# A gain row spread by TensorE, loads in fixed order and zero products in the opening stage of a hybrid decoder layer

## The chip, the cores and the metric

The kernel runs on one core of one Trainium2 chip. The metric is the device time of one execution in microseconds (us). TensorE does the matrix products, VectorE (DVE) and ScalarE (ACT) the elementwise work, GpSimd (POOL) a few small steps, SyncE (SP) issues most of the loads and stores.

## The reference, cut to what matters

The layer takes x, 1024 tokens by 1024 features, in float32. Only its beginning is touched by the change.

```
h    = rms_norm(x, norm_mix_pre)          # x * rsqrt(mean(x*x) + 1e-6) * gain
proj = h @ w_in                           # q, k, v | B, C, xc | g_att, g_conv
y_att  = stick_breaking_attention(q, k, v) @ w_att_branch
y_conv = (B * causal_dwconv(C * xc)) @ w_conv_branch
x = x + rms_norm((sigmoid(g_att)*y_att + sigmoid(g_conv)*y_conv) @ w_out, norm_mix_post)
# then a convolutional feed-forward part with norms of its own (w_up, w_down)
```

The columns of `w_in` for v are 512; for each of q and k they are 512 as well.

## The kernel before, in words

Float32 operands are represented by pairs of float16 numbers: a high half, and a low half that holds what the high half leaves out. One exact product of such pairs is made of three float16 products: high by high, high by low and low by high (`PASSES`). Before a tensor is split it is multiplied by a power of two, so that it fits float16. For weights the power comes from the sum of squares of the weight: `scale_of` adds up the partial sums, a product with a matrix of ones (into tile `pr`, line 76) spreads the total over the partitions, and three small DVE instructions make the power (lines 78 to 81). For the normalised input the power comes from the largest gain (`gain_max`, line 187, and `gain_pow2`, lines 194 to 197).

The opening stage of `mixer` works on eight token tiles of 128 tokens (tt = 0 to 7, called x0 to x7 as loads) and on four weight tiles of v (`st[0]` to `st[3]`, called v0 to v3 as loads; 128 by 1024 float32, 512 KB each). For a token tile the steps are:

- `load_x`: a DMA from SP's queue, 512 KB.
- `square_x`: ACT squares and sums (line 58); `rstd_x`: one DVE instruction (line 181) and a power on POOL (line 182).
- `norm_x`: DVE multiplies the tile by its reciprocal root and by the gain (line 359). The gain is `gb`, a 128 by 1024 tile that a DMA fills by reading the gain's 4 KB row once for each partition (line 407, 512 KB written).
- `turn_x`: eight transposes of 128 by 128 on TensorE into PSUM (line 364). The PSUM pool for them has two buffers.
- `high` (ACT, line 367) and `low` (DVE, line 370): the two halves of the turned tile, written to `hT`. "high(3)" is that step for token tile 3.

For v: ACT and DVE square the four weight tiles (`sm_v`; lines 58 and 480), `scale_of` gives the scale, `w_high` (ACT, line 431) and `w_low` (DVE, line 434) make the two halves `wv`, and `v_pass` (line 427) issues the products for a token tile into a PSUM bank `pv`. `v_out` evicts such a bank. Inside the stage the weights of q and k are begun too: `square_w` loads and squares them, `open_w` takes the scale and casts them. The first q and k products (`pq`, `pk`, line 211) end the stage; the attention stage follows, and after it the gates, the output projection and the feed-forward part.

The order of TensorE, DVE and ACT instructions in the opening stage and in the attention stage is the order in which the program names them (`tc.manual_schedule`, lines 466 and 918). Outside those stretches, and on SP before the change, a planner in the compiler chooses the order by priorities and a timeline that it simulates. Each engine runs its queue in order. SP's loads stand in the queue as x0, the gain, v0, x1, v1, v2, v3, x2, x3, two small weights of the convolutions, x4 to x7.

## Time and profile before

| what | us |
|---|---|
| median of 3 runs | 1352.25 |
| lowest and highest of them | 1351.61, 1354.85 |
| the profiled execution, whole | 1350.92 |
| the profiled execution, its span from first to last instruction | 1349.2 |

The profile is of one execution. Times in its rows are counted from the span's start. In a row of the timeline the columns are: start, duration, engine, line of the program and operation, the tile written and the tiles read with their shapes, a count, and in brackets how long the engine had been idle before and what ended the wait. PE is TensorE's product, PEld its weight load, SPq an issue of a DMA on SP's queue. A row of the windows holds the stretch, its length, the busy time (with the number of instructions) of PE, PEld, DVE, ACT and POOL, the granted TensorE clock, the share of time in which the DMA engines were busy, and GB/s.

### The profile page before, as it was taken

Reading aid. Unit: us, or ns where it says so; the run is one execution under the profiler, and the core shown is the slowest. Engines: PE = TensorE matmul, PEld = TensorE weight load, DVE = VectorE, ACT = ScalarE, POOL = GpSimd, SP = SyncE. Lnnn points to the kernel's source line nnn. Section 1 sums busy time; section 2 is a strip of 40 time slices with the busy share of each in tenths; the row PEclk is TensorE's granted clock in tenths of the full one; section 3 lists DMA queues with packets and bytes.
Section 4 is the critical chain, followed back from the end, with each engine's and each line's share of the span. In section 5 each row is a group of like instructions: output and inputs, shape, how many; then the busy total and the mean of one; then the engine's idle time right before and its main releaser. Section 6 shows DMA issues by size and latency. Waiting matters only on the chain. (4 is left out here: it accounts for less than half of the span.)

```text
span 1349.2 us, 16783 instructions
## 1 busy us (share of the span) xinstructions
PE 1311.9 (97%) x6491; PEld 590.0 (44%) x6491; DVE 1050.8 (78%) x1697; ACT 859.1 (64%) x1205; POOL 34.5 (3%) x58
## 2 busy tenths in 40 slices
PE   5999999999998999999999999999999999999997
PEld 3544444344433444444444444444444444444443
DVE  6568887878878957878788977975894896699855
ACT  6578877877777966665555676743752762576524
POOL 2000000000000000000110000000000000000002
PEclk9999999999999999999999999999999999999999
DMA  7011201101001222241431123222220312313126
GB/s 267 33 33 32 63 32 32 36 28 48 32 16 32 63 63 66 76 177 57 137 114 44 51 63 126 63 63 94 63 94 1 125 63 63 125 34 123 63 48 109
DMA packets 26608, 96.12 MB, mean 71 GB/s; under 512 B 3088, under 2 KB 3216, under 8 KB 26528
## 3 DMA queue, kind: packets, MB, share of 16 engines
q1 hardware_dynamic: 25088, 89.80, 20.2%
q0 software_dynamic: 1440, 5.24, 2.1%
q8 instruction: 51, 0.84, 0.3%
q14 instruction: 29, 0.24, 0.1%
HBM read 86.61 MB, written 8.42 MB: 70 GB/s over the span
## 5 line engine op out<-in xcount | busy, mean ns | idle before, releaser
L1538 PEld LDWEIGHTS <-wh_u 128*128 128x128 f16 x1848 | 178.8, 98 | 217.6 <-issue 3.8
L1312 PE MATMUL pd<-wdh,f 128*128 128x512 f16 (+1 forms) x1068 | 230.2, 377 | 2.7 <-ACT wdh L97 1.1
L1312 PEld LDWEIGHTS <-f 128*128 128x128 f16 x1068 | 104.5, 98 | 126.9 <-issue 4.0
L97 ACT ACTIVATE wh_u<-ws_u,sc 128x1024 f16<-128x1024 f32 (+1 forms) x66 | 64.7, 999 | 103.6 <-DVE sc L80 80.0
L1319 DVE SCALAR_TENSOR_TENSOR yacc<-pd,sd,yacc 128x512 f32<-128x512 f32 (+1 forms) x81 | 58.6, 742 | 73.4 <-PE pd L1312 65.9
L1538 PEld LDWEIGHTS <-wh_g 128*128 128x128 f16 x588 | 56.9, 98 | 68.7 <-issue 0.4
L1123 PE MATMUL py<-wh_wo,m 128*128 128x512 f16 x384 | 83.9, 379 | 0.0
L98 DVE SCALAR_TENSOR_TENSOR wh_u<-ws_u,sc,wh_u 128x1024 f16<-128x1024 f32 (+1 forms) x66 | 72.4, 1103 | 9.5 <-ACT wh_u L97 9.4
L824 ACT ACTIVATE sh<-sp 128x1024 f16<-128x1024 f32 (+3 forms) x48 | 40.4, 841 | 53.4 <-DVE sp L819 53.1
L1615 DVE SCALAR_TENSOR_TENSOR ugu<-cgu,cw_g,ugu 128x1023 f32<-128x1023 f32 (+1 forms) x44 | 56.4, 1283 | 11.3 <-ACT ugu L1613 10.9
L828 DVE TENSOR_TENSOR sh<-sp,sh 128x1024 f16<-128x1024 f32 (+3 forms) x48 | 45.9, 956 | 18.0 <-ACT sh L824 17.8
L1615 DVE SCALAR_TENSOR_TENSOR ua<-cau,cw_a,ua 128x1023 f32<-128x1023 f32 (+1 forms) x44 | 56.3, 1280 | 1.4 <-ACT ua L1613 1.3
L1123 PEld LDWEIGHTS <-m 128*128 128x128 f16 x384 | 37.5, 98 | 44.1
L819 DVE TENSOR_TENSOR sp<-A,sp 1x1024 f32<-1x1024 f32 (+3 forms) x40 | 35.9, 897 | 25.4 <-PE A L781 21.7
L850 ACT ACTIVATE w<-e 128x1024 f16<-128x1024 f32 (+3 forms) x48 | 40.5, 843 | 21.3 <-DVE e L845 20.4
L854 DVE SCALAR_TENSOR_TENSOR w<-e,w 128x1024 f16<-128x1024 f32 (+3 forms) x48 | 45.8, 954 | 9.2 <-ACT w L850 9.2
L814 ACT ACTIVATE sp<-e,one 128x1024 f32<-128x1024 f32 (+3 forms) x48 | 44.4, 925 | 6.0 <-DVE e L809 3.1
L845 DVE TENSOR_TENSOR e<-e,g 128x1024 f32<-128x1024 f32 (+3 forms) x48 | 45.7, 953 | 1.9 <-ACT g L841 1.8
L58 ACT ACTIVATE jk_u<-ws_u 128x1024 bf16<-128x1024 f32 x44 | 46.4, 1054 | 0.8
L756 PE MATMUL pywc<-p,wh_wc 128*128 128x512 f16 x192 | 43.2, 379 | 3.5 <-ACT sga L730 1.1
L211 PE MATMUL pcb<-hT,wh_cb 128*128 128x512 f16 x192 | 44.9, 379 | 0.9 <-DVE sc_cb L89 0.8
L800 ACT ACTIVATE e<-z,cz 128x1024 f32<-128x1024 f32 (+3 forms) x48 | 43.0, 897 | 3.6 <-PE z L781 3.6
(697 smaller groups left out, 2623.3 us busy)
## 6 DMA issues: line engine op xcount, KB each, us to landing
ws_u<-w_up_nt SPq DMA_DIRECT2D x44, 512.0 KB
ds<-w_down SPq DMA_DIRECT2D x22, 512.0 KB
wd<-w_down SPq DMA_DIRECT2D x22, 512.0 KB
ws_g<-w_in_nt SPq DMA_DIRECT2D x14, 512.0 KB
x<-x SPq DMA_DIRECT2D x8, 512.0 KB
ws_wo<-w_out SPq DMA_DIRECT2D x8, 512.0 KB
xr<-x SPq DMA_DIRECT2D x8, 512.0 KB
out<-x SPq DMA_DIRECT2D x7, 512.0 KB
```

Of the source, the lines that this page charges most:

```text
L58: self.nc.scalar.activation(self.junk(f"jk_{name}"), src, AF.Square, accum_out=acc)
L97: self.nc.scalar.activation(dst[:, 0, :], src, AF.Copy, scale=s)
L98: self.nc.vector.scalar_tensor_tensor(dst[:, 1, :], src, s, dst[:, 0, :], ALU.mult, ALU.subtract)
L211: nc.tensor.matmul(ps, w[:, wi, ds(k * P, P)], hT[:, hi, k, ds(c * NH, NH)], start=n == 0, stop=n == last)
L828: nc.vector.tensor_tensor(sh[:, 1, :, off:], u["sp"][:, :, off:], sh[:, 0, :, off:], ALU.subtract)
L845: nc.vector.tensor_tensor(e[:, :, off:], e[:, :, off:], u["g"][:, :, off:], ALU.mult)
L854: nc.vector.scalar_tensor_tensor(w[:, 1, :, off:], u["e"][:, :, off:], 2.0 ** 14, w[:, 0, :, off:], ALU.mult, ALU.subtract)
L1123: nc.tensor.matmul(ps, m16[k][:, hi, ds(tt * P, P)], wo[k][:, wi, sl], start=k == 0 and p == 0, stop=k == 7 and p == 2)
L1312: nc.tensor.matmul(pd[nh], f16[g][k][:, hi, ds(tt * P, P)], w[k][:, wi, ds(*part)], start=run is runs[0] and n == 0, stop=run is runs[-1] ...
L1319: nc.vector.scalar_tensor_tensor(y[:, sl], ps, sm[:, 0:1], y[:, sl], ALU.mult, ALU.add)
L1538: nc.tensor.matmul(ps, w[wt][:, wi, ds(wc * NH + k * P, P)], self.block(i, hi, k), start=first and n == 0, stop=n == 3 * KH - 1, skip_grou ...
L1615: nc.vector.scalar_tensor_tensor(u[:, lag:], c[:, :T - lag], sm[:, 2 - lag:3 - lag], u[:, lag:], ALU.mult, ALU.add)
```

## The change

- The gain's row goes to one partition (`g_row`, 4 KB, a DMA on ACT's queue, ahead of ACT's table load). TensorE spreads it over 128 partitions by two float32 products with a row of ones into a PSUM tile `gp`, which takes one of the two buffers for turned tiles. The norms of token tiles 0 and 1 read `gp`; the others read `gb` as before.
- The powers of two of the gain are made on one partition and spread by a further product (`ps2`).
- SP's loads get a fixed order, and the broadcast into `gb` stands behind x2.
- `warm(n)` issues n products of zeros, 128 by 512, into a bank that nobody reads: 3 ahead of turn 0, 1 on each side of turn 1, 4 behind the product of v's scale.
- The squares of v2 and v3 are split between ACT (first 512 columns) and DVE (the others).
- The high half of the first weight tile is cast in two halves, and the products of the high weight halves are put in another order (token tile 1's products with its low half one weight later).
- The cast of the constant `tri` moves from the start of the program to between low(0) and low(1).
- The products of token tiles 2 and 3 are cut in two: the first 12 of the 24 stand ahead of the q weight's or the k weight's scale product.

```diff
-            nc.scalar.preload_act_table_set("natural_log_exp_and_others")
...
-            nc.vector.tensor_copy(self.tri, tri32)
+            self.tri32 = tri32
...
+                gr = self.slot([P, D], F32, "g_row")
+                nc.scalar.dma_start(gr[0:1], a["g_mix_pre"])
+                nc.scalar.preload_act_table_set("natural_log_exp_and_others")
+                wz = self.slot([P, NH], F16, "wz")
+                nc.vector.memset(wz, 0.0)
+                on1 = self.slot([P, P], F32, "on1")
+                nc.vector.memset(on1[0:1], 1.0)
...
-                    nc.vector.scalar_tensor_tensor(xt[tt], xt[tt], rt[tt], gb, ALU.mult, ALU.mult)
+                    nc.vector.scalar_tensor_tensor(xt[tt], xt[tt], rt[tt], gp if tt < 2 else gb, ALU.mult, ALU.mult)
...
+                wm = pm.tile([P, NH], F32, tag="pm", name="warm")
+                def warm(n):
+                    for _ in range(n):
+                        nc.tensor.matmul(wm, wz[:, :P], wz, start=True, stop=True)
+                spq.enter_context(tc.manual_schedule(engines={ET.SP}))
                 load_x(0)
-                nc.sync.dma_start(gb, a["g_mix_pre"].broadcast_to([P, D]))
...
                 load_x(2)
+                nc.sync.dma_start(gb, a["g_mix_pre"].broadcast_to([P, D]))
                 load_x(3)
...
+                    gs = self.small("g_pre", keep=True)
+                    nc.vector.tensor_reduce(gs[0:1, 0:1], gr[0:1], AX.X, ALU.max, apply_absolute_value=True)
+                    self.gain_pow2(gs, 2, slice(0, 1))
+                    g16 = self.smp.tile([P, 2], BF16, tag="g16", name="g16", bufs=1)
+                    nc.vector.tensor_copy(g16[0:1], gs[0:1, 3:5])
+                    gp = ptp.tile([P, KD, P], F32, tag="pt", name="g_ps").rearrange("p k t -> p (k t)")
+                    for c in range(2):
+                        nc.tensor.matmul(gp[:, ds(c * NH, NH)], on1[0:1, :], gr[0:1, ds(c * NH, NH)], start=True, stop=True)
+                    ps2 = pm.tile([P, NH], F32, tag="pm", name="g2")
+                    nc.tensor.matmul(ps2[:, 0:2], self.ones[0:1, :], g16[0:1], start=True, stop=True)
+                    warm(3)
                     square_x(0)
                     rstd_x(0)
                     norm_x(0)
                     turn_x(0)
-                    g_sm = self.gain_max(gb, "pre")
+                    nc.vector.tensor_copy(gs[:, 3:5], ps2[:, 0:2])
+                    s_h, inv_h = gs[:, 3:4], gs[:, 4:5]
                     self.sumsq(st[0], sm_v[:, 0:1], "v_0")
                     square_x(1)
-                    s_h, inv_h = self.gain_pow2(g_sm, 2)
                     self.sumsq(st[1], sm_v[:, 1:2], "v_1")
                     rstd_x(1)
                     norm_x(1)
+                    warm(1)
                     turn_x(1)
+                    warm(1)
+                    h0, h1 = slice(0, NH), slice(NH, D)
+                    self.nc.scalar.activation(self.junk("jk_v_2a")[:, h0], st[2][:, h0], AF.Square, accum_out=sm_v[:, 2:3])
+                    square_v(2, 3, h1)
                     high(0)
-                    nc.vector.scalar_tensor_tensor(self.slot([P, D], F32, "jk_v_2"), st[2], 1.0, st[2], ALU.mult, ALU.mult,
-                                                   accum_out=sm_v[:, 2:3])
-                    self.sumsq(st[3], sm_v[:, 3:4], "v_3")
+                    square_v(3, 5, h1)
+                    self.nc.scalar.activation(self.junk("jk_v_3a")[:, h0], st[3][:, h0], AF.Square, accum_out=sm_v[:, 4:5])
                     high(1)
-                    s_v, inv_wv = self.scale_of(sm_v, 4, keep=True)
+                    s_v, inv_wv = self.scale_of(sm_v, 6, keep=True)
+                    warm(4)
                     low(0)
+                    nc.vector.tensor_copy(self.tri, self.tri32)
                     low(1)
                     for i in range(4):
-                        w_high(i)
+                        if i == 0:
+                            for c in range(2):
+                                w_high(i, c * NH, NH)
+                        else:
+                            w_high(i)
                         if i == 2:
                             square_x(2)
-                        for tt in range(2):
-                            v_pass(tt, (2 * i, 2 * i + 1), ((0, 0), (1, 0)), first=i == 0)
+                        ks = (2 * i, 2 * i + 1)
+                        v_pass(0, ks, ((0, 0),), first=i == 0)
+                        v_pass(1, ks, ((0, 0),), first=i == 0)
+                        v_pass(0, ks, ((1, 0),))
+                        if i:
+                            v_pass(1, (2 * i - 2, 2 * i - 1), ((1, 0),))
+                    v_pass(1, (6, 7), ((1, 0),))
...
                     square_w(2, "k")
+                    v_pass(2, range(4), PASSES, first=True)
                     lq = open_w(1, "q")
...
-                    v_pass(2, range(8), PASSES, first=True, last=True)
+                    v_pass(2, range(4, 8), PASSES, last=True)
...
                     lq()
+                    v_pass(3, range(4), PASSES, first=True)
                     lk = open_w(2, "k")
...
-                    v_pass(3, range(8), PASSES, first=True, last=True)
+                    v_pass(3, range(4, 8), PASSES, last=True)
```

More of the change, by code (lines that the diff above doesn't have):

```diff
@@ L188, in gain_max, with gain_pow2 @@
         return sm
-    def gain_pow2(self, sm, slack=0):
+    def gain_pow2(self, sm, slack=0, r=slice(None)):
         nc = self.nc
         si = sm.bitcast(I32)
-        nc.vector.tensor_scalar(sm[:, 1:2], sm[:, 0:1], 2.0 ** -100, None, ALU.max)
-        nc.vector.tensor_scalar(si[:, 2:3], si[:, 1:2], 0x7F800000, None, ALU.bitwise_and)
-        nc.vector.tensor_scalar(si[:, 3:4], si[:, 2:3], -1, (263 - slack) << 23, ALU.mult, ALU.add)
-        nc.vector.tensor_scalar(si[:, 4:5], si[:, 2:3], 1, -((9 - slack) << 23), ALU.mult, ALU.add)
+        nc.vector.tensor_scalar(sm[r, 1:2], sm[r, 0:1], 2.0 ** -100, None, ALU.max)
+        nc.vector.tensor_scalar(si[r, 2:3], si[r, 1:2], 0x7F800000, None, ALU.bitwise_and)
+        nc.vector.tensor_scalar(si[r, 3:4], si[r, 2:3], -1, (263 - slack) << 23, ALU.mult, ALU.add)
+        nc.vector.tensor_scalar(si[r, 4:5], si[r, 2:3], 1, -((9 - slack) << 23), ALU.mult, ALU.add)
         return sm[:, 3:4], sm[:, 4:5]
@@ L404, in v_mm @@
                         yield
+                wm = pm.tile([P, NH], F32, tag="pm", name="warm")
+                def warm(n):
+                    for _ in range(n):
+                        nc.tensor.matmul(wm, wz[:, :P], wz, start=True, stop=True)
+                spq = ExitStack()
+                ET = mybir.EngineType
+                spq.enter_context(tc.manual_schedule(engines={ET.SP}))
                 load_x(0)
-                nc.sync.dma_start(gb, a["g_mix_pre"].broadcast_to([P, D]))
                 st = [self.ws.tile([P, D], F32, tag="ws", name=f"ws_v_{i}") for i in range(4)]
@@ L416, in mixer @@
                 nc.sync.dma_start(self.cfw, a["conv_ffn"])
+                for tt in range(4, 8):
+                    load_x(tt)
+                spq.close()
                 wv = [self.wh.tile([P, 2, D], F16, tag="wh", name=f"wh_v_{i}") for i in range(4)]
                 sm_v = self.small("sm_v")
-                ET = mybir.EngineType
                 pv = [None] * 4
@@ L428, in v_pass, with w_high @@
                                          start=first and n == 0, stop=last and n == len(todo) - 1)
-                def w_high(i):
-                    nc.scalar.activation(wv[i][:, 0, :], st[i], AF.Copy, scale=s_v)
+                def w_high(i, *part):
+                    sl = ds(*part) if part else slice(None)
+                    nc.scalar.activation(wv[i][:, 0, sl], st[i][:, sl], AF.Copy, scale=s_v)
                 def w_low(i):
@@ L462, in run, with square_v @@
                         next(gen)
-                for tt in range(4, 8):
-                    load_x(tt)
                 with tc.manual_schedule(engines={ET.PE, ET.DVE, ET.Activation}):
+                    gs = self.small("g_pre", keep=True)
[9 more added lines that the diff above has]
+                    warm(3)
+                    jv = self.slot([P, D], F32, "jk_v_2")
+                    def square_v(i, c, sl):
+                        nc.vector.scalar_tensor_tensor(jv[:, sl], st[i][:, sl], 1.0, st[i][:, sl], ALU.mult, ALU.mult,
+                                                       accum_out=sm_v[:, c:c + 1])
                     square_x(0)
```

## The prediction

> **What bounds the kernel now.** I read the page first (busy shares, slices), then busy time by windows, then the timeline of the first 60 us engine by engine.

> ```profile
> span 1349.2 us, 16783 instructions
> ...
> PE 1311.9 (97%) x6491; PEld 590.0 (44%) x6491; DVE 1050.8 (78%) x1697; ACT 859.1 (64%) x1205; POOL 34.5 (3%) x58
> ```
> ```profile
> 0.00:16.78 16.78, 4.10 (x17) 3.38 (x18) 8.29 (x22) 10.23 (x15) 3.76 (x18) 1.00 0.91 332
> 16.78:62.00 45.22, 44.12 (x224) 22.49 (x224) 29.83 (x53) 25.99 (x39) 6.15 (x6) 1.00 0.30 100
> 62.00:160.00 98.00, 98.00 (x550) 41.25 (x549) 74.17 (x141) 73.67 (x102) 0.00 (x0) 1.00 0.13 39
> ```

> The first time after the window's length is TensorE's (PE). It is busy 97% of the span. Its widest gap lies ahead of 16.78 us (4.10 of 16.78 us busy); from there to 160 us it lacks 1.1 us. The edited stage is therefore worth what it takes off TensorE's start, off its slow products and off its waits up to about 44 us; from 62 to 160 us there is no idle time in which a gain could vanish.

> ```profile
> 7.99 1.97 PE L364 MATMUL pt_pre<-ident,x 128*128 128x128 f32 x8 [7.99 <-DVE x L359]
> 12.57 1.97 PE L364 MATMUL pt_pre<-ident,x 128*128 128x128 f32 x8 [2.62 <-DVE x L359]
> ...
> 16.78 9.83 PE L427 MATMUL pv<-wh_v,hT 128*128 128x512 f16 x36 [1.97 <-ACT wh_v L431]
> 26.45 1.04 PE L364 MATMUL pt_pre<-ident,x 128*128 128x128 f32 x8
> 27.32 2.75 PE L427 MATMUL pv<-wh_v,hT 128*128 128x512 f16 x12
> ...
> 31.93 0.16 PE L76 MATMUL pr<-rb,ones 128*128 128x1 bf16 x1 [0.98 <-DVE rb L73]
> 31.95 5.34 PE L427 MATMUL pv<-wh_v,hT 128*128 128x512 f16 x24
> ...
> 44.16 5.34 PE L211 MATMUL pq<-hT,wh_q 128*128 128x512 f16 x24
> ```
> ```profile
> 20.15 0.15 PEld L427 LDWEIGHTS <-hT 128*128 128x128 f16 x1 [0.28 <-issue]
> 20.57 5.54 PEld L427 LDWEIGHTS <-hT 128*128 128x128 f16 x26 [0.28 <-issue]
> ```

> From 16.78 to 44.16 us TensorE works without a break but for one wait of 0.98 us at 31.93. Up to 20.57 us the weight loads stand about 0.42 us apart, after it 26 of them take 5.54 us, 0.213 each. So the first nine products run at half rate for (20.57 - 16.78) = 3.79 us and lose 9 x (0.421 - 0.213), about 1.9 us. The windows' granted clock (third number from the end) says 1.00 throughout and does not show this; the spacing does.

> What holds the start to 16.78:

> ```profile
> 4.36 1.06 ACT L58 ACTIVATE jk_n_pre<-x 128x1024 bf16<-128x1024 f32 x1 [2.27 <-DMA x<-x]
> ...
> 7.95 1.06 ACT L58 ACTIVATE jk_v<-ws_v 128x1024 bf16<-128x1024 f32 x1 [2.44 <-DMA ws_v<-w_v]
> ...
> 13.07 1.06 ACT L58 ACTIVATE jk_v<-ws_v 128x1024 bf16<-128x1024 f32 x1 [0.41 <-DMA ws_v<-w_v]
> 14.03 0.18 ACT L58 ACTIVATION_READ_ACCUMULATOR jk_v<-ws_v 128x1 f32 x1
> 14.58 1.11 ACT L367 ACTIVATE hT<-pt_pre,g_pre 128x1024 f16<-128x1024 f32 x1 [0.36 <-PE pt_pre L364]
> 15.59 3.21 ACT L431 ACTIVATE wh_v<-ws_v,sc 128x1024 f16<-128x1024 f32 x3
> ```
> ```profile
> 5.85 0.55 POOL L182 TENSOR_TENSOR r_pre<-r_pre,neghalf 128x1 f32<-128x1 f32 x1 [2.44 <-DVE r_pre L181]
> 6.65 1.28 DVE L359 SCALAR_TENSOR_TENSOR x<-x,r_pre,g_pre 128x1024 f32<-128x1024 f32 x1 [0.96 <-DMA g_pre<-g_mix_pre]
> 7.85 1.21 DVE L187 TENSOR_REDUCE g_pre<-g_pre 128x1 f32<-128x1024 f32 x1
> ...
> 14.25 0.16 DVE L70 TENSOR_REDUCE sc<-sm_v 128x1 f32<-128x4 f32 x1 [0.59 <-ACT jk_v L58]
> ...
> 15.12 0.14 DVE L81 TENSOR_SCALAR sc<-sc 128x1 int32<-128x1 int32 x1
> 15.18 2.47 DVE L370 SCALAR_TENSOR_TENSOR hT<-pt_pre,g_pre,hT 128x1024 f16<-128x1024 f32 x2
> ```

> The waits that end on a DMA give landings: x0 4.36, the gain's broadcast 6.65, first v weight (v0) 7.95, last v weight (v3) 13.07. From there the chain is: sum of squares (to 14.21), scale (14.25 to 15.26, DVE), while ACT casts token tile 1 until 15.6, then the high half of the first weight, then TensorE.

> **The change part by part.**

> *Loads.* The 512 KB broadcast leaves its place between x0 and v0 and goes behind x2. It held the queue from 4.36 to 6.65, 2.29 us; the four loads behind v0 (x1, v1, v2, v3) took (13.07 - 7.95)/4 = 1.28 each. So v3 lands between 1.28 us (one tile's share) and 2.29 us earlier. I take 1.9, nearer to what the wait showed: 11.15. The broadcast then lands at about 11.15 + 1.28 + 2.29 = 14.7, and its first reader, the norm of token tile 2, comes near 19.4: covered by 4.7 us.

> *The gain row.* A 4 KB load on ACT's queue replaces it for tiles 0 and 1. Another 4 KB transfer, the table load and the first and last of the four powers-of-two steps:

> ```profile
> 0.80 1.28 ACT L247 ACT_TABLE_LOAD   x1 [0.80 <-PEq L1660]
> ...
> 9.10 0.15 DVE L194 TENSOR_SCALAR g_pre<-g_pre 128x1 f32<-128x1 f32 x1
> ...
> 9.55 0.14 DVE L197 TENSOR_SCALAR g_pre<-g_pre 128x1 int32<-128x1 int32 x1
> ...
> 36.70 0.57 SPq L300 DMA_DIRECT2D vr<-v  x2
> ...
> 38.38 0.52 SPq L302 DMA_DIRECT2D v<-vr  x2
> ```

> The second pair waits for the first to land: 1.7 us from issue. ACT's first slot is at 0.80 us and an issue takes about 0.4, so the row lands near 2.9 us if it is served at once, or at 4.36 if it is served behind x0. ACT's table load then follows the issue and ends near 2.5, ahead of ACT's first work at 4.36: free. The two spreading products have no f32 row but the turns: 1.97/8 = 0.25 us per 128 columns, so 0.98 per 512 and 1.97 for both. The ends are 0.84 (f16 pace) and 3.9 (twice the turn). The spread is ready at 4.9, at worst 6.8 for a row at 2.9. The reciprocal root (5.85 + 0.55 = 6.40) decides the first norm, at about 6.6 as before. Reduction (1.21) and powers of two with their cast (9.10 to 9.69 and 0.15, so 0.75) run on DVE ahead of it, done near 5.0; before, they took 1.8 us of DVE behind it. Queued behind the row on DVE is everything, on TensorE everything: that is the exposed new wait. Reading the spread from PSUM costs nothing (L370 reads PSUM in 1.24, L359 reads SBUF in 1.28). The spread holds one of two turning buffers until the norm of tile 1 has read it, for which turn 1 waits anyway.

> *Squares split.* v2 and v3 are squared half on ACT, half on DVE. A 128x512 pass of ACT is seen below at 0.59. After high(0), v3's half runs 11.6 to 12.4 with its accumulator read, against 14.21. The scale is ready 1.05 later (14.21 to 15.26 before), at 13.45; high(1) on ACT fills 12.4 to 13.5; the first weight's half cast takes 0.6 instead of 1.14. First real product: 14.1 by this sum. The four zero products issued ahead of it take 0.85 us at full rate, 1.7 at half rate, and start only after the scale's own product near 13.1: free in the first case, start 14.85 in the second. I take 14.3. Gain at the start 16.78 - 14.3 = **2.5**.

> *Rate.* Spread, zero products and two turns keep TensorE at work from about 3 us with short holes. If the full rate is on by 14.3, the nine slow products go: **1.9**. [...]

> *Order of products.*

> ```profile
> 29.57 0.59 ACT L377 ACTIVATE v<-pv 128x512 f16<-128x512 f32 x1
> ...
> 32.51 1.15 ACT L448 ACTIVATE wh_q<-ws_q,sc 128x1024 f16<-128x1024 f32 x1 [1.31 <-DVE sc L80]
> 33.56 1.10 ACT L367 ACTIVATE hT<-pt_pre,g_pre 128x1024 f16<-128x1024 f32 x1
> 34.69 1.28 DVE L370 SCALAR_TENSOR_TENSOR hT<-pt_pre,g_pre,hT 128x1024 f16<-128x1024 f32 x1 [2.16 <-ACT hT L367]
> ```

> The first 12 products of token tile 2 move ahead of the q weight's scale product: the wait of 0.98 at 31.93 is filled: **1.0**. Price: the scale on DVE, then the casts of q and of tile 3 on ACT and low(3) on DVE queue behind that product, which now stands behind 12 others. From 14.3 on, 48 products of 0.216, two turns of 0.87 (26.45 to 27.32), 12 products more and 0.2 of waiting bring TensorE to it at 14.3 + 7.8 + 1.7 + 2.6 + 2.6 + 0.2 = 29.2; scale 0.6, cast 1.05, high(3) 1.1 and low(3) 1.28 end at 33.3. TensorE reaches tile 3's products after 12 products and a turn, at 32.7, and has two that need only the high half: it waits 0.2. At full rate TensorE also overtakes ACT's second weight cast: 13.5 + 0.6 + 0.55 + 1.1 = 15.75 against 14.3 + 6 x 0.213 = 15.6, wait 0.2. The cast of tri (DVE, about 0.25, between low(0) and low(1)) is covered by some 1 us; without cover it costs 0.25. With 0.2 for what I can't see, new waits cost **0.6**, from 0.4 to 1.2.

> *Sum.* 2.5 + 1.9 + 1.0 - 0.6 = 4.8 us: q's first product at 39.4 instead of 44.16. Norms and casts stay ahead of it by 0.3 us or more in this count, thin at turns 3 and 6. The attention stage keeps its written order and shifts as a block. The profiled execution took 1350.92 us (1.72 around its span): 1346.1 after. The median of the runs shown is 1352.25, 1.3 above, so **1347.5** as a median.

> **Rivals.**

> *Turns do not open the rate.* For: two turns of 1.97 us each stood before 16.78 and the products still began slow. Against: 2 us of idleness lay between. Then only the zero products around turn 1 (from 12.6) count, full rate comes at 12.6 + 3.79 = 16.4, the start is 14.85, four slow products lose 0.85, one wait vanishes: gain 3.7, 1348.5. [...] Chance 0.13.

> *Zero products open nothing.* Start 14.85, nine slow products as before: the gain is 1.9 + 1.0 - 0.25 = 2.7, 1349.6. Chance 0.11; nothing in this trace multiplies zeros.

> *The later order moves.* Behind the attention stage the order comes from the compiler's planner, which sees other times at the front. Idle TensorE time there is the yardstick:

> ```profile
> 640.00:720.00 80.00, 77.56 (x390) 38.76 (x389) 67.74 (x119) 48.81 (x95) 12.02 (x16) 1.00 0.35 119
> 720.00:800.00 80.00, 77.12 (x360) 34.83 (x360) 69.90 (x108) 48.27 (x64) 0.00 (x0) 1.00 0.17 53
> ```

> 5.3 us idle in 160; a shuffle could add or remove about half, plus or minus 2.7: 1344.8 to 1350.2. Chance 0.14.

> *The gain row lands late (slower).* DVE's first waiting instruction, the row's reduction, holds the whole in-order engine. From landing L the first norm comes at L + 3.0 (reduction 1.21, powers 0.75, the root's two steps, DVE's before 5.85, POOL's, and the gap to the norm, 1.1). The second norm follows 2.5 later (1.28, a copy, the root's steps), and its end, turn 1, high(1) and the half cast take 1.28 + 1.97 + 1.1 + 0.6 more: start = first norm + 7.5 at the soonest, 14.1 from 6.6. So each us beyond L = 3.6 costs one. At L = 4.36, behind x0, it costs 0.8; at 8.4 the gain is gone; at 13, behind the 512 KB loads ahead of v3, the kernel is 4.6 slower, 1356.9. For: the DMA engines are busy 0.91 of the first window. Against: the row is 4 KB on a queue of its own and issued as early as x0. Chance 0.07, about half of it past break-even.

> **How the numbers follow.** Forecast 0.55, its own range 1346.5 to 1348.5. One measurement of this kernel tells 0.3% (4.1 us) from no change. The forecast's 4.8 lies barely above it: nine tenths of its weight counts as faster, with half of the reshuffle 0.55; both clock rivals and most of the rest fall within, 0.39; slower, 0.06, is half of the late row and the worst shuffles. The range 1344.5 to 1350.8 holds the forecast, both clock rivals and most of the reshuffle.

> **What would show it.** Right: the last v weight's squares start near 11.5 on ACT; first product over wh_v at 14.1 to 14.9, spaced 0.213; no wait at q's scale product; pq near 39.4; the same shift at 62 and 160 us. Wrong: spacing of 0.42 after the start (clock rivals), the first norm later than 7 us (row or spread late), waits on low(3) or on turn 6 above 0.5 us, or a shift that is lost behind the attention stage.

## The result, and the profile after

| kernel | median, us | lowest to highest | runs | ratio to the kernel before |
|---|---|---|---|---|
| before | 1351.69 | 1350.38 to 1354.85 | 9 | 1 |
| changed | 1348.11 | 1346.11 to 1350.34 | 9 | 0.997 (0.996 to 0.9981) |

The median of the changed kernel is 3.6 us lower, where 4.8 had been forecast: 0.27% by the medians, and the interval of the ratio lies below 1. Its nine times stand in three groups: 1346.11 to 1346.56 (four), 1348.11 and 1348.20, 1349.86 to 1350.34 (three). The profiled execution is from the last group (1350.34, span 1348.6), so its trace has to be read with that in mind.

TensorE in the opening of the changed kernel (timeline, then its weight loads):

```profile
3.31 3.75 PE L490 MATMUL g_ps<-g_row,on 1*128 1x512 f32 x4 [3.31 <-DMA g_row<-g_mix_pre]
...
8.49 1.97 PE L370 MATMUL pt_pre<-ident,x 128*128 128x128 f32 x8
...
11.67 1.94 PE L370 MATMUL pt_pre<-ident,x 128*128 128x128 f32 x8 [0.78 <-DVE x L365]
...
13.90 1.87 PE L416 MATMUL warm<-wz 128*128 128x512 f16 x4
15.56 8.51 PE L444 MATMUL pv<-wh_v,hT 128*128 128x512 f16 x36
...
30.84 0.17 PE L76 MATMUL pr<-rb,ones 128*128 128x1 bf16 x1
30.86 2.75 PE L444 MATMUL pv<-wh_v,hT 128*128 128x512 f16 x12
...
34.32 2.98 PE L444 MATMUL pv<-wh_v,hT 128*128 128x512 f16 x12
...
40.63 5.34 PE L211 MATMUL pq<-hT,wh_q 128*128 128x512 f16 x24
...
57.34 0.34 PE L830 MATMUL z<-q,k 64*128 64x128 f16 x6 [0.54 <-DVE k L339]
```
```profile
16.42 0.15 PEld L444 LDWEIGHTS <-hT 128*128 128x128 f16 x1 [0.28 <-issue]
16.79 6.79 PEld L444 LDWEIGHTS <-hT 128*128 128x128 f16 x32 [0.22 <-issue]
...
34.97 1.84 PEld L444 LDWEIGHTS <-hT 128*128 128x128 f16 x10 [0.55 <-DVE hT L376]
```

The first real product starts at 15.56 instead of 16.78. About three products, not nine, are slow: from 16.79 on, 32 weight loads take 6.79 us. The wait ahead of q's scale product (row 30.84) is gone. Instead a weight load waits 0.55 us for low(3); the products behind it lose some 0.2 us by that (12 of them take 2.98 us at 34.32, against 2.75 at 30.86). q's first product is at 40.63, 3.53 us earlier than 44.16; the first `z` of attention is at 57.34, against 60.43 in the kernel before, and this 3.1 us stays through attention (last `A` at 408.08, against 411.20). At the end of the span only 0.6 us of it is left (1348.6 against 1349.2).

What happened behind attention is in the windows (columns as in the rows of before; the third number from the end is the granted clock):

```profile
405.85:409.26 3.41, 1.18 (x5) 0.48 (x5) 2.25 (x3) 3.21 (x6) 0.00 (x0) 1.00 0.27 112
409.26:412.67 3.41, 3.41 (x9) 1.21 (x8) 2.54 (x9) 1.97 (x2) 0.00 (x0) 0.50 0.00 0
716.46:719.87 3.41, 1.51 (x7) 0.63 (x7) 3.27 (x6) 2.82 (x5) 0.00 (x0) 1.00 0.01 2
719.87:723.28 3.41, 3.41 (x10) 1.22 (x9) 3.24 (x6) 2.34 (x5) 0.00 (x0) 0.50 0.00 0
```

Twice the clock falls to 0.50 for exactly one stretch of 3.41 us, each time behind a stretch in which TensorE was busy less than half. (Here and below, falls behind the last product are left aside: the kernel before has one at 1345.03 and the changed kernel one at 1344.51, 2.8 and 2.9 us behind the end of the last product, and they hold no product up.) The waits that make those stretches stood in the kernel before as well, and no stretch at half clock follows them there:

```profile
408.08 1.16 PE L830 MATMUL A<-sh,tri 128*128 128x512 f16 x4 [3.05 <-ACT g L890]
```
```profile
411.20 1.16 PE L781 MATMUL A<-sh,tri 128*128 128x512 f16 x4 [3.04 <-ACT g L841]
```
```profile
406.37:409.78 3.41, 1.78 (x9) 0.68 (x7) 2.66 (x3) 3.38 (x6) 0.00 (x0) 1.00 0.47 137
409.78:413.19 3.41, 1.99 (x9) 0.87 (x9) 2.61 (x6) 2.93 (x5) 0.00 (x0) 1.00 0.06 22
```

In the kernel before, the 3.04 us wait lies astride two stretches and neither is emptier than 1.78 us. The second wait, 1.79 us ahead of `pu0c`, lies astride two stretches there as well (716.99 to 720.40 with 2.22 us busy, 720.40 to 723.81 with 2.61).

### The profile page after: what moved, and what is told of

It reads as the page before. It is cut to its first block, busy times and chain, and to the rows that moved or that the text cites. A ratio compares the mean times of both kernels' runs of the same rounds, so it can differ in the third digit from the quotient of the medians.

```text
span 1348.6 us, 16828 instructions
## 1 busy us (share of the span) xinstructions
PE 1321.1 (98%) x6505; PEld 592.6 (44%) x6505; DVE 1051.4 (78%) x1703; ACT 859.5 (64%) x1208; POOL 34.4 (3%) x58
## 5 line engine op out<-in xcount | busy, mean ns | idle before, releaser
L58 ACT ACTIVATE jk_u<-ws_u 128x1024 bf16<-128x1024 f32 x44 | 46.4, 1054 | 0.8
L211 PE MATMUL pcb<-hT,wh_cb 128*128 128x512 f16 x192 | 44.9, 380 | 0.9 <-DVE sc_cb L89 0.8
```

The source lines that it names most:

```text
L58: self.nc.scalar.activation(self.junk(f"jk_{name}"), src, AF.Square, accum_out=acc)
L211: nc.tensor.matmul(ps, w[:, wi, ds(k * P, P)], hT[:, hi, k, ds(c * NH, NH)], start=n == 0, stop=n == last)
```

## The experiments

Twelve kernels ran, in three groups, each group on one chip with the kernel before (medians 1351.22, 1351.38 and 1351.66 us).

**The zero products.** Without them:

```diff
-                        nc.tensor.matmul(wm, wz[:, :P], wz, start=True, stop=True)
+                    pass
```

> The changed kernel without any of the nine zero products. Theory A (zero products help to open the full rate): the first real product comes at about 15.3, freed from the four zero products ahead of it, but the rate rises 3.4 to 6.8 us after that, so 8 to 16 products run at 0.427 us instead of about 2; q's first product at 41.6 to 43.2 against 40.6, and the median 1.0 to 2.5 us above the changed kernel's 1348.1. Theory B (zero products count for nothing): the rate rises at the same time as with them, near 16.4, q's first product at 40.3 to 40.6, median within 0.5 us of the changed kernel.

Measured: 1348.77 us, ratio 0.9982 (0.9972 to 0.9992). The interval overlaps that of the changed kernel (0.996 to 0.9981), so by the times alone a gain of the zero products is not shown.

```profile
15.06 9.28 PE L440 MATMUL pv<-wh_v,hT 128*128 128x512 f16 x32 [1.69 <-ACT wh_v L445]
```
```profile
19.04 0.15 PEld L440 LDWEIGHTS <-hT 128*128 128x128 f16 x1 [0.28 <-issue]
19.43 4.63 PEld L440 LDWEIGHTS <-hT 128*128 128x128 f16 x22 [0.24 <-issue]
```

The start is no later (15.06), but the products are slow up to 19.43, and q's first product lies 26.71 us behind the start instead of 25.07. This is one profile, and the opening of the changed kernel itself varies between profiles (below). What zero products do is seen best in the changed kernel's own profile, in the stretch behind which its clock opened at 16.73:

```profile
13.32:16.73 3.41, 3.41 (x11) 1.22 (x10) 2.74 (x7) 3.08 (x4) 0.00 (x0) 1.00 0.98 368
```

Zero products are busy in 2.37 of these 3.41 us. All other products of the stretch come to 1.7 us at most, less than the 2.63 us of the stretch ahead of it (9.91 to 13.32), behind which the clock did not open. So in this trace the products of zeros counted.

**More of them** (18 instead of 4 ahead of the first real product):

```diff
-                    warm(4)
+                    warm(18)
```

> The changed kernel with 18 instead of 4 zero products ahead of the first real one. Theory A (zero products count as work): the spacing of the zero products themselves falls from 0.427 to 0.213 us within the 18, at the latest 6.8 us after they begin, and all real products run at 0.213 from the first on. Theory B: all 18 stand 0.427 us apart (7.7 us) and the first 8 to 16 real products are slow too.

Measured: one time, 1348.25. The clock was already open at 12.23, so the 18 took 4.04 us and held the first real product to 16.48; q's first product came at 40.98. This one time shows nothing won beyond what four do.

**The loads.** The second x block right behind the first, and the broadcast back in its old place:

```diff
                 load_x(0)
+                load_x(1)
...
-                        load_x(1)
```

> The changed kernel with x1 loaded directly behind x0 and squared ahead of the first v weight. Theory A (the landing of x1 at 8.24 sets the start, by way of norm 1 and turn 1): x1 lands near 5.8, norm 1 starts near 9.3 instead of 10.24, first real product near 14.7 instead of 15.56, median about 0.9 us lower. Theory B (ACT's row of squares behind the third landing sets it, by way of the scale): norm 1 comes earlier all the same, but the last squares end near 13.1 as before, first real product at 15.3 to 15.6, median within 0.4 us.

```diff
                 load_x(0)
+                nc.sync.dma_start(gb, a["g_mix_pre"].broadcast_to([P, D]))
...
-                nc.sync.dma_start(gb, a["g_mix_pre"].broadcast_to([P, D]))
```

> The changed kernel with the broadcast put back between x0 and the first v weight; the norms of tiles 0 and 1 still read the spread row. By the forecast's own step the last v weight lands 1.9 us later than in the changed kernel and the start moves as much: first real product at 17.3, median 1.5 to 2 us up. Rival (in the changed kernel ACT's squares, not the last landing, end last): the last squares start near 13.1 instead of 12.42, first real product near 16.2, median 0.5 to 0.8 us up.

Measured: 1347.9 us, ratio 0.9969 (0.9958 to 0.9981), with x1 early; 1350.3, ratio 0.9988 (0.9979 to 0.9997), with the broadcast first. By the ratios the broadcast's later place is worth 0.0018, 2.4 us (0.9988 against the changed kernel's 0.997, whose intervals just overlap). With the broadcast first the first real product came at 16.54, between what the forecast's step (17.3) and its rival (16.2) had said; its profile has three stretches at half clock, one of them in the opening (13.49 to 16.91), so part of the 2.4 us can be the clock's. With x1 early the start was at 13.74, earlier than theory A had it, but the median is only 0.2 us below the changed kernel's, as theory B had it. q's first product came at 38.63, 5.5 us earlier than before, and yet the span was only 3.1 us shorter (1346.1): at 406.09 and 716.70 two stretches at half clock begin, as in the changed kernel.

**No spread.** Loads as in the last one, and both first norms read the broadcast tile:

```diff
-    nc.vector.scalar_tensor_tensor(xt[tt], xt[tt], rt[tt], gp if tt < 2 else gb, ALU.mult, ALU.mult)
+    nc.vector.scalar_tensor_tensor(xt[tt], xt[tt], rt[tt], gb, ALU.mult, ALU.mult)
...
-    nc.tensor.matmul(gp[:, ds(c * NH, NH)], on1[0:1, :], gr[0:1, ds(c * NH, NH)], start=True, stop=True)
```

> The changed kernel with the broadcast of g_pre back between x's first block and w_v, and with both first norms reading the broadcast tile: TensorE spreads no row. Beside it stands the kernel with the same loads that still spreads the row (1350.3, first real v product 16.54, q's first product 41.22). Theory A (the spread itself gains nothing; it only frees the broadcast's place in the queue): 1350.3 within 0.5, first product within 0.3 of 16.5. Theory B (the spread's 3.75 us at TensorE hold the first norm and turn): first norm 0.5 us earlier at 6.65, first product 16.0, median 1349.8. Theory C (its products are work that opens the clock): clock open later than 16.9, q's first product 42.5 or more, median 1351.5.

Measured: 1350.3 us, ratio 0.9989 (0.998 to 0.9998); first real product 16.36, both as theory A had them; q's first product 41.81. No gain of the spread as such shows; what it does is free the broadcast's place in the queue. The clock opened at 18.29, later than theory C's 16.9, but q's first product came earlier than its 42.5.

**The cut of v(2) and v(3).** Taken out of the changed kernel, and alone in the kernel before:

```diff
-                    v_pass(2, range(4), PASSES, first=True)
...
-                    v_pass(2, range(4, 8), PASSES, last=True)
+                    v_pass(2, range(8), PASSES, first=True, last=True)
```

> The changed kernel with v(2) and v(3) in one piece of 24 products each, at their old places, instead of cut in two halves around opening q's and k's weights. Theory A (the prediction's step: the cut fills a wait of TensorE worth 1.0 us): q's first product 1.0 us later than the changed kernel's 40.6, at 41.6, and the median 1.0 us up, 1349.1. Theory B (the cut only moves the wait to low(3), 0.55 us): 0.4 us later, median 1348.5.

> The kernel before with v(2) and v(3) cut in two halves around opening q's and k's weights, and nothing else of the change. From the start of the real v products to q's first product the kernel before took 27.38 us; the changed order without the cut took 25.92 and with it 24.89 at the same full rate. Theory A (the cut fills 1.0 us of waiting by itself): 26.35 us from start to q's first product, median 1.0 us below the kernel before, 1350.4. Theory B (it only pays when the products run at full rate): 27.1 us or more, median 1351.2.

Measured without the cut: 1351.41 us, ratio 0.9995 (0.9986 to 1.0004). Its start was 15.13 and q's first product 41.05, so 25.92 us between them against 24.89 in the runs below that have the same full rate and the cut: the cut fills 1.03 us. The larger loss comes later. In its profile the last `A` still starts 3.1 us earlier than in the kernel before (408.06 against 411.20), but the first product of `pywa`, the next tile, starts 1.0 us later (448.90 against 447.86):

```profile
423.31 1.06 ACT L58 ACTIVATE jk_wa<-ws_wa 128x1024 bf16<-128x1024 f32 x1 [1.68 <-DMA ws_wa<-wa]
```
```profile
426.38 5.96 PE L803 MATMUL pywc<-p,wh_wc 128*128 128x512 f16 x19 [3.34 <-DVE ywc L809]
```

In this kernel the compiler has put one square of the branch weights (`jk_wa`) between two evictions at the end of attention. It waits for its load, TensorE waits 3.34 us for what queues behind it, and the next stretch, 426.6 to 430.0, is at half clock. Neither theory had that.

Measured with the cut alone: 1350.73 us, ratio 0.9995 (0.9987 to 1.0004), which by itself is not apart from no change. The wait ahead of the scale product is gone, and 25.90 us lie between start (16.76) and q's first product (42.66) instead of 27.38, less than either theory said. By estimate some 0.5 of the 1.48 come from an opening of the clock 1.0 us earlier (19.64 against 20.66; half of it at the half rate); without that it would be 26.4, the figure of theory A. Its times stand in three groups, and each has its own mean granted clock: five of 1349.56 to 1350.11 at 0.999, three of 1350.73 to 1351.20 at 0.997, three of 1353.17 to 1353.63 at 0.995. The first five lie 1.1 us below the 13 runs of the kernel before that have 0.998 or 0.999 (medians 1349.81 and 1350.88), as theory A had it; chosen afterwards, these runs are a hint and no proof.

**The two late waits filled.** Twelve products of a zero operand ahead of the last `A`, eight repeated ones into `pu0c` ahead of its first real product:

```diff
+                    if k == nu - 1:
+                        for _ in range(12):
+                            mm(self.zps, self.tri, self.z16.broadcast_to([P, NH]), start=False, stop=False)
                     at(sums, k)
...
+        z = 8 if self.name == "u0" and i == 5 else 0
+        for m in range(z):
+            nc.tensor.matmul(ps, w[0][:, 0, ds(0, P)], l.hA[:, 0, 0, ds(0, NH)], start=True, stop=True, skip_group_check=True)
```

> The changed kernel, with zero or repeated products laid into two later waits of TensorE: twelve products of a zero operand into the open bank pywc just before the last A (the wait of 3.05 us at 405.0 to 408.1), and eight repeated products into bank pu0c before its first real product, whose start resets them (the wait of 1.79 us at 716.4 to 718.2). Twenty products of 0.213 us, all inside the waits, so nothing is delayed. Theory A (each wait lets the granted clock fall to half for 3.41 us in some runs, and each such stretch costs about 1.8 us, which makes the steps of 1346.1 to 1346.6, 1348.1 to 1348.2 and 1349.9 to 1350.3 between runs): no stretch at half clock between 20 and 1340 us, the runs draw together at 1346.0 to 1347.0, median 1346.4. Theory B (the steps come from the landing of the first loads, the clock's fall is only seen beside them): median 1348, runs as wide as before, although no stretch at half clock is left. Theory C (the products delay A or pu0c): median 1348.5 or more.

Measured: 1346.82 us (1346.34 to 1348.0, five runs), ratio 0.9965 (0.9953 to 0.9978). Its opening, which is the same code but for one small memset, and its two late places:

```profile
2.29 3.75 PE L492 MATMUL g_ps<-g_row,on 1*128 1x512 f32 x4 [2.29 <-DMA g_row<-g_mix_pre]
...
14.13 0.38 PE L446 MATMUL pv<-wh_v,hT 128*128 128x512 f16 x1 [0.30 <-ACT wh_v L451]
...
39.02 5.34 PE L211 MATMUL pq<-hT,wh_q 128*128 128x512 f16 x24
...
406.47 1.16 PE L833 MATMUL A<-sh,tri 128*128 128x512 f16 x4 [0.44 <-ACT g L893]
```
```profile
400.00:420.00 20.00, 18.73 (x92) 7.67 (x91) 15.50 (x25) 12.15 (x17) 0.00 (x0) 1.00 0.12 35
715.00:725.00 10.00, 9.73 (x46) 4.26 (x45) 7.60 (x14) 6.12 (x10) 0.00 (x0) 1.00 0.01 2
```

No stretch at half clock is left, and the group near 1350 is gone, as theory A had it. The runs are still 1.7 us wide, though the mean granted clock is 0.999 in all five. And the opening differs by 1.4 us from that of the first profile although nothing in it was changed: the row landed at 2.29 instead of 3.31, and the clock was open at 9.88 instead of 16.73.

> The changed kernel itself once more, for a second profile of its opening and more times beside the others of this group. The kernels with filled waits, whose opening is the same code, had their first real v product at 14.13 and q's first product at 39.02, and their clock open at 9.88, where the changed kernel's profile had 15.56, 40.63 and 16.73. Theory A (the opening is a draw: where the loads land and where the clock's stretches of 3.41 us begin): the clock opens either near 10 or near 16.7; with 10 the first product lies at 14.1 to 15.2 and q's at 39.0 to 40.1; times 1346 to 1350.5 in steps, median 1347.5 to 1348.5. Theory B (the filled kernels differ at their start by their order of instructions): again 15.5 and 40.6, median 1348.1 or more.

Measured: 1348.62 us (1345.91 to 1349.68, seven runs), ratio 0.9974 (0.9963 to 0.9986). A third draw of the same opening: row at 2.31, clock open at 14.54, first real product 14.61, q's first product 39.43, and both late stretches at half clock again (span 1347.1):

```profile
403.66:407.07 3.41, 0.36 (x3) 0.19 (x2) 2.21 (x3) 3.38 (x7) 0.00 (x0) 1.00 0.41 154
407.07:410.49 3.42, 3.42 (x9) 1.13 (x8) 2.54 (x7) 2.82 (x4) 0.00 (x0) 0.50 0.00 0
714.28:717.69 3.41, 1.44 (x10) 0.86 (x9) 2.83 (x5) 1.91 (x4) 0.00 (x0) 1.00 0.00 0
717.69:721.10 3.41, 3.39 (x9) 1.16 (x9) 3.41 (x6) 2.96 (x6) 0.00 (x0) 0.50 0.01 2
```

The opening time of this third draw, 14.54, is neither of the two that theory A had foreseen; that the opening is a draw holds.

**The same fill elsewhere.** In the kernel before, and with x1 early (with both fills, then with the first alone; the edits are those above):

> The kernel before with the same twenty products in the same two later waits, and nothing else. Theory A (the kernel before loses by the same fall of the clock in some of its runs, 1350.1 to 1354.9): median 1350.2, runs drawn together at 1349.8 to 1350.8. Theory B (its phase leaves it undisturbed, as its profiled execution shows, and its width is from elsewhere): 1351.3, no change. So by A the change itself is worth the difference of the two filled kernels, 1350.2 to 1346.4 = 3.8 us; by B some of the fill's gain in the changed kernel is a loss that the change had brought.

> The changed kernel with the second x block loaded right behind the first and squared ahead of w_v's first part, and with the same twenty products in the two later waits. Theory A: the early opening (10.1 us) and the earlier q product (38.6 us) are no longer paid back at 406 and 717 us: median 1344.5, runs 1344.0 to 1345.5. Theory B (what the second block gains is lost behind attention by something else than the clock): median 1347 to 1348, as with the early second block alone (1347.9).

> The changed kernel with the early second x block and with the twelve zero products before the last A, but without the eight in bank pu0c. Theory A (the eight products keep the clock open at 717): a stretch at half clock near 717 in the profile or in part of the runs, median 1347.5. Theory B (they are of no use, and their 0.5 us at 1114 is saved): no such stretch, median 1346.1, against 1346.6 with them.

Measured: the kernel before, filled, took 1353.01 us (1351.83 to 1353.32), ratio 1.001 (1.0001 to 1.0019): slower, which neither theory had. On the clock theory A was right. Of the 21 runs of the kernel before in this group, seven have a mean granted clock of 0.995 to 0.997 and times of 1352.11 to 1354.62; the other 14 have 0.998 or 0.999 and 1350.15 to 1352.05. All eleven of the filled kernel have 0.998 or 0.999. So, as the mean clock has it, the kernel before falls to half rate in some of its runs too, and the fill takes that away; but the filled kernel lies some 2 us above the undisturbed runs. In its profile the clock opened at 22.60, 1.9 us later than the 20.66 of the kernel before (the first 36 products of v, from 16.69, took 10.84 us against 9.83); its last `A` was 1.2 us later (412.44 against 411.20) and its span 2.3 us longer (1351.5). DVE and ACT have some instructions in another order behind attention than without the fill. Of the 2.3 us, 0.9 are there at the first `z`, 1.2 at the last `A`, and 0.6 are lost between 1100 and 1160 us, where the changed kernel with the same eight products loses 0.5 as well. Why its times lie 1.6 us higher as a whole isn't settled.

With x1 early and both fills: 1346.64, ratio 0.9965 (0.9951 to 0.9978), two us above what was expected. With the first fill alone: 1345.75 us (1345.66 to 1348.44), ratio 0.9961 (0.9948 to 0.9974), span 1344.0, no half-clock stretch in its profile (the emptiest one near 717, 714.20 to 717.62, has 1.58 us busy), as theory B had it, though two of five times lie 1.6 us or more above the others. This is the fastest kernel of the study; beside the changed kernel of the same group it is 2.9 us lower in the median, but the intervals of the two ratios overlap, so that it beats the changed kernel is likely and not shown.

## Why the prediction was right, and where it was not

**Start (forecast 14.3, gain 2.5).** Three draws of the same code: 15.56, 14.61, 14.13, gains of 1.2, 2.2 and 2.7. Two terms were mis-sized. The spread took 3.75 us, not 1.97; the upper bound of 3.9 was the nearer end. The row landed at 2.3 to 3.3 around the forecast 2.9. In the first profile the first norm waited for the spread and came at 7.16, 0.5 us late and past the 7 us that the prediction had named as a sign of being wrong; in the two others it came at 6.70 and 6.56. Yet the start lost little by it, since the second x block landed late in the first profile and turn 1 waited for that, not for the spread:

```profile
7.16 1.28 DVE L365 SCALAR_TENSOR_TENSOR x<-x,r_pre,g_ps 128x1024 f32<-128x1024 f32 x1 [1.34 <-PE g L492]
```
```profile
8.24 1.06 ACT L58 ACTIVATE jk_n_pre<-x 128x1024 bf16<-128x1024 f32 x1 [1.30 <-DMA x<-x]
...
12.42 0.62 ACT L518 ACTIVATE jk_v_3a<-ws_v 128x512 bf16<-128x512 f32 x1
...
14.66 3.40 ACT L449 ACTIVATE wh_v<-ws_v,sc 128x512 f16<-128x512 f32 x4
```

The last half square came at 12.42 there, forecast 11.6; with the second x block landing earlier it came at 11.53 and 11.64. And in the first profile the four zero products ran at half rate (1.87 us), the case that the prediction had priced at a start of 14.85.

**Rate (1.9).** About 1.3 in the first profile, where the clock opened at 16.73, behind the start at 15.56; all of 1.9 in the two others, where it was open before the first real product (14.54 before 14.61, 9.88 before 14.13). That the full rate would be on by 14.3 was an estimate that no run had shown; of the three profiles one has it so.

**Wait filled (1.0) and new waits (0.6).** The cut's 1.03 is measured. From start to q's first product the time fell from 27.38 to 24.89 in the filled kernel, 2.49 = 1.9 + 1.0 - 0.4. The products lose 0.2 on low(3), as forecast, though the weight load waits 0.55; the wait on the second cast is 0.24 in the filled kernel, where 0.2 was forecast, and none in the first profile. Another 0.4 goes between q's first product and the first `z`, which waits 0.54 us for DVE's k; the prediction had no term for that. New waits are thus 0.6 to 0.9, inside the 0.4 to 1.2.

**q's first product (39.4).** 40.63, 39.43, 39.02. The sum was right for the opening, within its variation from profile to profile.

**"The attention stage shifts as a block."** It does. The step that failed is the one behind it: the prediction let the shift run to the end, with a rival for another order of instructions. How far TensorE is ahead of the kernel before, at the first product of a tile, shows where the shift goes (all in us, from the profiles):

| place | in the kernel before, at | first profile | second profile | both waits filled | x1 early, first wait filled |
|---|---|---|---|---|---|
| first `z` | 60.43 | 3.09 | 4.29 | 4.70 | 4.85 |
| first `pywa`, behind attention | 447.86 | 2.48 | 3.75 | 4.72 | 4.83 |
| first `pu1c`, behind the second wait | 721.22 | 2.84 | 4.08 | 5.62 | 5.16 |
| first `pu0b`, the tile behind it | 726.54 | 1.16 | 2.43 | 5.62 | 5.16 |
| end of the last product | 1342.20 | 0.64 | 1.99 | 4.54 | 5.05 |
| late stretches at half clock | 0 | 2 | 2 | 0 | 0 |

The stretch behind attention costs 0.5 to 0.6 us, the one behind the second wait 1.7, and not 1.8 each as had been expected of the fill. Where no such stretch is, the shift that attention has is still there at the end, within 0.2 us. So the other order cost next to nothing here, and the two half-rate stretches took what is missing. Of the 5.62 us that both fills have at 721 us, 1.1 are gone at the end; 0.5 of that go between 1100 and 1160 us, where the kernel with the first fill alone loses nothing.

This is shown for the profiled executions. The three groups of the nine times are not simply none, one and two such stretches. In the profiles the mean granted clock of a run is 0.998 or 0.999 without a stretch at half clock, 0.998 with one, 0.996 with two and 0.995 with three. The times near 1350 and those near 1348 all have 0.996, so two stretches fit both groups, and what parts them is more likely the opening: the profiled runs of 1350.34 and 1348.77 us have two stretches each and are 1.2 us apart at the first `z`. The four fastest have 0.997 to 0.999; the two at 0.997 lie below every profile without a stretch, so they seem to have had one as well. That the median came within 0.6 us of the forecast is therefore partly luck: the sum has no term for the late stretches, and the nine times lie 4.2 us apart.

**Rivals.** Turns counted for the rate. In the filled kernel the clock opened at 9.88, behind the stretch of turn 0, and two thirds of that stretch's busy time are the turn (1.97 of 2.96):

```profile
6.47:9.88 3.41, 2.96 (x12) 1.76 (x10) 1.93 (x4) 2.79 (x6) 0.61 (x2) 1.00 1.03 419
```

Without the turn 1.0 us of work would be left in it, less than the 2.63 us behind which the clock stayed at half in the changed kernel's first profile. That zero products open nothing is refuted by the stretch from 13.32 to 16.73 above, 2.37 of whose 3.41 us are zero products. The late row did not come: 3.31 at the latest, below the 3.6 from which it was to cost; only with the long spread behind it did it hold the first norm, by 0.5 us. The other order of instructions decided once, in the kernel without the cut.

## What to carry to other kernels

Two of TensorE's waits (3.04 and 1.79 us) had no stretch at half rate behind them in the trace of before; once the work ahead of them was shifted, each was followed by 3.41 us at half clock, which cost 0.5 to 0.6 and 1.7 us. So list TensorE's long waits behind an edit, compare the mean granted clock of the runs when times stand in steps (here 0.996 to 0.999), and try to fill the waits with idle products. Each fill has to be judged by itself: here the first one was enough in the fastest kernel, and some of the time that the second one gained was lost again later. A gain in the opening must be followed in two or three profiles of the same code, since the landing of the row (2.29 to 3.31) and the opening of the clock (9.88 to 16.73) differed between three profiles of the same opening. A reordering at one place is only judged when the order of all engines behind it is compared as well.

## What the hardware showed that was not expected

```profile
16.23:19.64 3.41, 2.88 (x7) 0.99 (x7) 2.60 (x3) 3.41 (x5) 0.00 (x0) 1.00 1.03 410
```
```profile
7.72:11.13 3.41, 2.74 (x11) 2.08 (x12) 2.26 (x5) 3.16 (x7) 0.55 (x1) 1.00 1.02 416
```
```profile
6.50:9.91 3.41, 3.37 (x12) 1.70 (x11) 1.50 (x3) 1.96 (x5) 0.28 (x2) 1.00 1.02 404
```

The rows are of the cut alone (opens at 19.64), of the second profile of the changed kernel (does not open at 11.13) and of its first profile (3.37 us busy, does not open at 9.91; 0.56 of it are the spread's products of one row, so these seem to count less). The other stretches ahead of an opening that were measured with 2.88 us or more and did not open the clock (2.92 to 3.41 us, in five other kernels and in both profiles of the changed one) have products of the spread in them too; no run isolates them.

It closed behind 0.36, 1.18, 1.44 and 1.51 us (the rows above) and stayed open behind 1.52 in the kernel without the spread:

```profile
407.41:410.82 3.41, 1.52 (x7) 0.67 (x7) 2.45 (x5) 2.93 (x5) 0.00 (x0) 1.00 0.18 73
```

One stretch does not fit: 406.13 to 409.54 in the kernel without the cut, 1.48 us busy (its last `A` starts at 408.06), was not followed by half clock. So no one figure parts the two cases in these records. The idle time of 1.79 us ahead of `pu0c`, with 0.2 more behind it, was enough in the changed kernel, where it fell into one stretch (716.46 to 719.87, 1.51 us busy).
